# General tiles for the transferred weight groups of a seven-product down projection, and half the finished blocks added to x in DRAM

## The chip, the cores and the metric

The kernel runs on one core of one Trainium2 chip. The metric is the device time of one execution in microseconds (us). The kernel before was timed in three runs: 789.63, 788.41 and 789.20 us, median 789.2. A separate execution, with the hardware profiler on, took 788.42 us; its span from the first to the last instruction is 786.6 us, at a mean granted TensorE clock of 0.99.

Engines: TensorE (PE in the profile; PEld are its weight loads), VectorE (DVE), ScalarE (ACT), GpSimd (POOL) and SyncE (SP). GpSimd and SyncE issue nearly all of the transfers in the part discussed here.

## The reference

One block of a hybrid network: 512 tokens, model width 1024, float32. A gated mix of an mLSTM and a block attention comes first and gives a new x; then follow a second norm and a gated feed-forward, and a last norm. Only the end matters here:

```python
h = modulate(rms_norm(x, norm2_g[l]), sh2, sc2)
f = jax.nn.silu(jnp.einsum('bsd,df->bsf', h, w_gate[l])) * jnp.einsum('bsd,df->bsf', h, w_up[l])
x = x + g2[:, None, :] * jnp.einsum('bsf,fd->bsd', f, w_down[l])
...
return rms_norm(x, normf_g)
```

f is 512 x 2816, w_down is 2816 x 1024.

## The kernel before

**Products in float32r.** Every product is made of three matmuls (`mm3`, L285 to L287): each operand is split into a rounded part ("hi", cast to float32r) and a remainder ("lo"), and hi.hi, hi.lo and lo.hi are accumulated in PSUM. For the weights that is `cvt` (ScalarE casts at L268, DVE subtracts at L270), for the moving or stationary activations `split` (ScalarE at L291, DVE at L292). A weight chunk arrives in a "raw" buffer (4 of them, `load`, SyncE, L182 and L187) and leaves as a pair of "whl" buffers (4 of them, so two chunks).

**Seven products.** Of the 22 row blocks of w_down, 16 are multiplied as a 2 x 2 block matrix in seven products in place of eight. `PRODUCTS = (1, 2, 5, 6, 3, 7, 4)` is their order. Each product has two weight groups of 128 x 2048 (1 MB), so there are 14 groups, g = 0 to 13. A group is 24 matmuls: two halves e (of tokens), four quarters k (512 columns of the group), three matmuls each. Products 5, 7, 6 and 4 need sums of weight blocks; those are made beforehand by DMA in DRAM (tiles `ws`). The other side needs sums of blocks of f, made by DVE (`sum1` to `sum4`) in place, and split group by group (`aparts`). The results sit in three pairs of PSUM banks (yb, xb2, zb): copies are kept (`keep`), finished blocks are summed (`summed`) and added onto x (`onto_x`): DVE scales the block by g2, and GpSimd issues a DMA that adds it to its destination.

**Transferred groups.** Four of the 14 groups (`BY_DMA`) take no part in `cvt`. GpSimd loads the weights with a DMA that rounds them to float32r (`rounded_load`, L217); ScalarE writes the negative of that into a second buffer (`remainder_load`, L223); GpSimd then lets a DMA add the weights once more onto that, which leaves the remainder (L225). In the kernel before these are groups 2, 5, 8 and 12. Both buffers come from the four "raw" ones. In the loop over groups, iteration g first issues `rounded_load(g + 3)` and then `remainder_load(g + 2)`; the load of group 2 stands inside the last gate/up chunk (L1561).

**Order.** The schedule is written by hand: each engine executes its instructions in the order in which the program issues them. In iteration g come the loads of groups g + 2 and g + 3, the two lines just named, and for each half e the entry of `hooks`, the splits and the cast for group g + 1, and the half's 12 matmuls. Tiles of one kind share a number of buffers; a new one takes the buffer that has been free longest, and its first writer waits for the last reader of the tile before. General tiles `T()` (128 x 512, 31 buffers) hold splits, kept copies, x's rows at the end and more; `X()` tiles (8 buffers) mostly hold blocks of f.

**x and the end.** x was written to DRAM earlier (`xkeep`). After the last gate/up chunk its eight quarter rows are fetched into general tiles (L1689), and all eight finished blocks are added onto those. Behind the seven products come six plain row blocks (`PLAIN`, three chunks of two, from `C_PL` on): 8 banks, 24 products of three matmuls a chunk. The first chunk runs whole, the other two are interleaved per output block with the residuals (L1803), the last norm and the stores. Their weights are multiplied by g2 first (`gate_weights`, L244). `fsplit(k)` makes the six splits of f for them; split 0 is made in group 13, 1 and 2 with the first chunk, 3 to 5 after it.

Of the kernel before, what the change touches and what calls it, by code (L numbers as in the profile page):

```python
# [14 lines left out]
ALU = mybir.AluOpType  # L15
# [96 lines left out]
def block_kernel(ctx, tc, x, wall, adaw, pcol, prow, positions, inv_freq, out):  # L112
# [82 lines left out]
    def operand(o, g):  # L195
        p = PRODUCTS[o]
        if p in wsum:
            return wsum[p][blk(g), :]
        return flat(wall, OFF_BLOCKS[{1: 0, 2: 2, 3: 3}[p]] + g * 128 * 2048, [[2048, 128], [1, 2048]])
# [10 lines left out]
    BY_DMA = (2, 5, 8, 12)  # L210

    def rounded_load(g):
        n = C_DN + g
        if g in BY_DMA:
            raws[n] = None
            parts[n] = tuple(wp.tile([128, RAW], F32R, tag="raw", name=nm("wd"), bufs=4)[:, :SIZES[n]] for _ in range(2))
            G.dma_start(parts[n][0], operand(*divmod(g, 2)))  # L217

    def remainder_load(g):
        if g in BY_DMA:  # L220
            hi, lo = parts[C_DN + g]
            for e in range(2):
                A.activation(lo[:, e * 1024:e * 1024 + 1024], hi[:, e * 1024:e * 1024 + 1024].bitcast(F32),  # L223
                             AF.Copy, scale=-1.0)
            G.dma_start(lo, operand(*divmod(g, 2)), accum_op=ALU.add)  # L225
# [1309 lines left out]
    def seven(n):  # L1535
# [24 lines left out]
        if not more:  # L1560
            rounded_load(2)  # L1561
            aparts(0)
# [123 lines left out]
    for i in range(NT):  # L1686
        for q in range(2):
            xr[i][q] = T()
            SP.dma_start(xr[i][q][:], xkeep[i][:, q * 512:q * 512 + 512])  # L1689
# [18 lines left out]
    def onto_x(name, e, i, q):  # L1708
        t = kept[name][e]
        if q:  # L1710
            V.scalar_tensor_tensor(out=t, in0=t, scalar=-1.0, in1=g2row[q][:, :512], op0=ALU.mult, op1=ALU.mult)
        else:
            V.tensor_tensor(out=t, in0=t, in1=g2row[q][:, :512], op=ALU.mult)
        G.dma_start(xr[i][q][:], t, accum_op=ALU.add)

    def pair():
# [11 lines left out]
        (8, 1): lambda: summed("m1", xb2, 0),  # L1728
        (9, 0): lambda: (onto_x("m1", 0, 0, 0), summed("m1", xb2, 1)),
        (9, 1): lambda: onto_x("m1", 1, 1, 0),  # L1730
        (10, 0): lambda: summed("u2", zb, 0),
        (10, 1): lambda: (onto_x("u2", 0, 0, 1), summed("u2", zb, 1)),
        (11, 0): lambda: onto_x("u2", 1, 1, 1),
        (11, 1): lambda: summed("m5", yb, 0),
        (12, 0): lambda: (summed("m5", yb, 1), onto_x("m5", 0, 2, 1)),
        (12, 1): lambda: gate_weights(C_PL, 0),
        (13, 0): lambda: (gate_weights(C_PL, 1), onto_x("m5", 1, 3, 1)),
# [3 lines left out]
    for g in range(groups):  # L1741
# [4 lines left out]
        rounded_load(g + 3)  # L1746
        remainder_load(g + 2)
        wh, wl = parts_of(n)
        for e in range(2):
            hooks.get((g, e), lambda: None)()  # L1750
            if g < groups - 1:
                aparts(2 * g + 2 + e)
            elif e == 0:
                fps[0] = fsplit(0)
            if g + 1 not in BY_DMA:
                cvt(n + 1, e)
            for k in range(4):
                ah, al = (v[:, k % 2, blk(e)] for v in ap[2 * g + k // 2])
                mm3(target[p][e][:], ah, al, wh[:, k, :], wl[:, k, :], p in (1, 2, 5) and g % 2 == 0 and k == 0,
                    g % 2 == 1 and k == 3, True)  # L1760
    nfrow = [T(), T()]
    for q in range(2):
        SP.dma_start(nfrow[q][:, :512], flat(prow, PB + 2 * D + q * 512, [[0, 128], [1, 512]]))
# [10 lines left out]
    for kk in range(2):  # L1774
        if kk:
            mid(C_PL)
        fps[kk + 1] = fsplit(kk + 1)
        for i in range(NT):
            for q in range(2):
                mm3(db[i][q][:], fps[kk][0][:, blk(i)], fps[kk][1][:, blk(i)], ch[0][:, kk, q * 512:(q + 1) * 512],  # L1780
                    ch[1][:, kk, q * 512:(q + 1) * 512], kk == 0, kk == 1 and (i, q) == (NT - 1, 1))
    root_table()
# [3 lines left out]
    for k in range(3, 2 * NP):  # L1786
        fps[k] = fsplit(k)
# [147 lines left out]
```

## Time and profile before

| | us |
|---|---|
| median of three runs | 789.2 |
| the profiled execution | 788.42 |
| its span | 786.6 |
| seven-product down projection (first to last matmul's start) | 648.17 to 742.88 |
| plain products, to the last matmul | 742.88 to 779.58 |

How to read the views used below. A row of the timeline has the start in us from the span's start, the duration, the engine, the line of the kernel, the operation, output<-input by the program's names, and in brackets the idle time before it and what ended that. Matmuls overlap: the distance of two starts is what one costs. A row of the waits has who waited for whom, us in total, times, and the longest. A row of busy time by stretches has from:to, length, each engine's busy time with its number of instructions, the granted clock of TensorE, the mean busy share of the 16 DMA engines, and GB/s. A row of a DMA queue has packets, MB and the time that its packets took as a share of 16 engines. The engines' idle time counts only where it ends last.

### The profile page before, as it was taken

What the parts mean: (1) busy time and instruction counts of PE and PEld (TensorE: products, weight loads), DVE (VectorE), ACT (ScalarE), POOL (GpSimd) and SP (SyncE); (2) the same over time, 40 slices, a digit from 0 to 9 for tenths busy, and PEclk for the clock granted to TensorE, in tenths of its full rate; (3) what the DMA queues carried; (4) which work ended last, traced back from release to release, by engine and by line L of the source; (5) the groups of instructions that cost most, each with busy time, mean ns of one, the idle gap of its engine ahead of it and who ended that gap; (6) DMA issues with size and microseconds to landing.
All of it is one profiled execution on the core that took longest, in us unless ns stands there. A gap on an engine that the chain in (4) does not pass through costs nothing.

```text
span 786.6 us, 12066 instructions
## 1 busy us (share of the span) xinstructions
PE 760.7 (97%) x4587; PEld 660.0 (84%) x4587; DVE 555.6 (71%) x879; ACT 389.3 (49%) x686; POOL 344.9 (44%) x447
## 2 busy tenths in 40 slices
PE   8999999999999999999999999999999999797986
PEld 7789988778887787788889999999999998575865
DVE  5677877665565544488647799898988877656765
ACT  6679743324454444322357545555554554464243
POOL 5484545999856878950002045453653000002200
PEclk9999999999999999999999999999999999898999
DMA  9954325435421422559326438363947456668812
GB/s 337 385 176 153 108 80 175 133 131 215 151 108 55 161 107 107 210 193 322 102 82 215 162 121 240 137 237 112 312 157 205 171 182 194 174 200 233 236 38 108
DMA packets 30041, 136.17 MB, mean 173 GB/s; under 512 B 4120, under 2 KB 4256, under 8 KB 17056
## 3 DMA queue, kind: packets, MB, share of 16 engines
q1 hardware_dynamic: 23680, 105.72, 37.0%
q0 software_dynamic: 4480, 27.26, 14.2%
q10 hardware_dynamic: 1824, 2.43, 1.2%
q8 instruction: 36, 0.59, 0.3%
q14 instruction: 21, 0.17, 0.1%
HBM read 127.01 MB, written 20.97 MB: 188 GB/s over the span
## 4 chain that ended last, share of the span: by engine, by line
PE 82%; DVE 7%; DMA 6%; ACT 2%; issue 2%; SPq 0%; ACTq 0%; DVEq 0%
PE psm L285 12%; PE psm L287 12%; PE psm L286 12%; PE psb L285 6%; PE psb L286 6%; PE psb L287 6%; PE psa L286 5%; PE psa L287 5%; PE psa L285 5%; DMA wd<-ws 2%; DMA t<-in_dram 2%; DVE whl L270 2%; PE psa L655 1%; PE psa L1156 1%; DVE whl L1506 1%
## 5 line engine op out<-in xcount | busy, mean ns | idle before, releaser
L270 DVE TENSOR_TENSOR whl<-raw,whl 128x1024 fp32r<-128x1024 f32 (+2 forms) x92 | 116.5, 1271 | 46.4 <-ACT whl L268 43.7
L268 ACT CAST whl<-raw 128x1024 fp32r<-128x1024 f32 (+2 forms) x91 | 92.6, 1034 | 51.4 <-DVE raw L244 18.7
L338 POOL TENSOR_TENSOR accp<-accp,prod 128x256 f32<-128x256 f32 x112 | 98.6, 880 | 9.3
L1500 ACT CAST whl<-raw 128x1024 fp32r<-128x1024 f32 x57 | 59.8, 1050 | 69.8 <-DVE raw L1490 47.0
L335 POOL TENSOR_SCALAR prod<-ada,cact 128x256 f32<-128x256 f32 x112 | 90.4, 807 | 0.1
L1506 DVE TENSOR_TENSOR whl<-raw,whl 128x1024 fp32r<-128x1024 f32 x57 | 72.6, 1275 | 16.1 <-ACT whl L1500 15.9
L285 PE MATMUL psa<-t,whl 128*128 128x256 f32 x276 | 79.0, 286 | 2.0 <-DVE f L1593 2.0
L287 PE MATMUL psa<-t,whl 128*128 128x256 f32 x276 | 78.1, 283 | 0.0
L286 PE MATMUL psa<-t,whl 128*128 128x256 f32 x276 | 78.1, 283 | 0.0
L285 PE MATMUL psm<-hh,whl 128*128 128x512 f32 x192 | 77.5, 404 | 0.5 <-ACT x L1138 0.5
L285 PE MATMUL psm<-t,whl 128*128 128x256 f32 (+1 forms) x256 | 76.2, 298 | 0.0
L286 PE MATMUL psm<-t,whl 128*128 128x256 f32 (+1 forms) x256 | 75.8, 296 | 0.0
L287 PE MATMUL psm<-t,whl 128*128 128x256 f32 (+1 forms) x256 | 75.8, 296 | 0.0
L287 PE MATMUL psm<-hh,whl 128*128 128x512 f32 x192 | 74.9, 390 | 0.0
L286 PE MATMUL psm<-hh,whl 128*128 128x512 f32 x192 | 74.9, 390 | 0.0
L285 PEld LDWEIGHTS psa<-t,whl 128*128 128x128 f32 x276 | 52.9, 192 | 2.7 <-DVE f L1593 2.6
L286 PEld LDWEIGHTS psa<-t,whl 128*128 128x128 f32 x276 | 53.0, 192 | 0.1
L287 PEld LDWEIGHTS psa<-t,whl 128*128 128x128 f32 x276 | 52.9, 192 | 0.0
L285 PEld LDWEIGHTS psm<-t,whl 128*128 128x128 f32 x256 | 49.0, 191 | 1.4 <-DVE x L1593 0.2
L286 PEld LDWEIGHTS psm<-t,whl 128*128 128x128 f32 x256 | 49.0, 191 | 1.3
L287 PEld LDWEIGHTS psm<-t,whl 128*128 128x128 f32 x256 | 49.0, 191 | 1.3
L335 POOL TENSOR_SCALAR accp<-ada,cact 128x256 f32<-128x256 f32 x16 | 12.1, 757 | 86.5 <-DMA ada<-in_dram 86.5
(493 smaller groups left out, 2045.3 us busy)
## 6 DMA issues: line engine op xcount, KB each, us to landing
raw<-in_dram SPq DMA_DIRECT2D x55, 1024.0 KB, 5.2
ada<-in_dram SPq DMA_DIRECT2D x16, 1024.0 KB, 4.8
ws<-in_dram POOLq DMA_DIRECT2D x6, 2048.0 KB, 14.4
t<-in_dram SPq DMA_DIRECT2D x32, 256.0 KB, 6.2
raw<-ws SPq DMA_DIRECT2D x6, 1024.0 KB, 6.8
ws<-ws POOLq DMA_DIRECT2D x2, 2048.0 KB, 12.2
wd<-in_dram POOLq DMA_DIRECT2D x4, 1024.0 KB, 6.5
wd<-ws POOLq DMA_DIRECT2D x4, 1024.0 KB, 7.9
```

Source lines behind the costliest of these rows:

```text
L268: (eng.tensor_copy if eng else A.copy)(hi[:, s], raws[n][:, s])
L270: (eng or V).tensor_tensor(out=lo[:, s], in0=raws[n][:, s], in1=hi[:, s].bitcast(F32), op=ALU.subtract)
L285: PE.matmul(o, lh, rh, start=start, stop=False, skip_group_check=again)
L286: PE.matmul(o, lh, rl, start=False, stop=False, skip_group_check=again)
L287: PE.matmul(o, ll, rh, start=False, stop=stop, skip_group_check=again)
L335: G.tensor_scalar(t[:], rv[:, k, :], cact[:, k:k + 1], 1.0, op0=ALU.mult, op1=ALU.mult)
L338: G.tensor_tensor(out=p[:], in0=p[:], in1=t[:], op=ALU.add)
L655: PE.matmul(g1[m][:], w[:, blk(m)], h[:], start=k == 0 and e == 0, stop=k == KD - 1 and e == 2)
L1156: PE.matmul(bs[e][:, o:o + n], qp[a][r, blk(i)], kp[b][r, :n], start=g == 0, stop=g == 2)
L1500: A.copy(hi, src)
L1506: V.tensor_tensor(out=lo, in0=src, in1=hi.bitcast(F32), op=ALU.subtract)
```

## The change

The transferred groups become 4, 7, 10 and 13. Each is held in eight general tiles (four quarters of the rounded part, four of the remainder) and transferred in quarters of 256 KB. The rounded load is issued at the head of iteration g - 4, the negation and the adding load in the second half of iteration g - 3. Group 2 is an ordinary group now, and the early load in the last gate/up chunk is gone. Of x's rows, two are fetched into `X()` tiles before the seven products, two in group 12, and four after the first plain chunk's first half; the four finished blocks of the first 256 tokens (m1 and u2) are added onto `xkeep` in DRAM, ahead of that fetch. The hooks of groups 8 to 13 are regrouped, and the splits for the plain products come one step earlier. The load of the last norm's row moves behind the fetch of x.

```diff
@@ -192,11 +192,12 @@
 
     wsum = {p: dq.tile([256, 2048], F32, tag=f"ws{p}", name=nm("ws")) for p in (5, 7, 6, 4)}
 
-    def operand(o, g):
+    def operand(o, g, k=None):
         p = PRODUCTS[o]
+        c, w = (0, 2048) if k is None else (k * 512, 512)
         if p in wsum:
-            return wsum[p][blk(g), :]
-        return flat(wall, OFF_BLOCKS[{1: 0, 2: 2, 3: 3}[p]] + g * 128 * 2048, [[2048, 128], [1, 2048]])
+            return wsum[p][blk(g), c:c + w]
+        return flat(wall, OFF_BLOCKS[{1: 0, 2: 2, 3: 3}[p]] + g * 128 * 2048 + c, [[2048, 128], [1, w]])
 
     def weight_sums():
         for p, q, b in ((5, None, (0, 0)), (7, None, (1, 1)), (6, 7, (0, 0)), (4, 6, (1, 0))):
@@ -207,22 +208,21 @@
 
     wsums = weight_sums()
 
-    BY_DMA = (2, 5, 8, 12)
+    BY_DMA = (4, 7, 10, 13)
+    cast = {}
 
     def rounded_load(g):
-        n = C_DN + g
         if g in BY_DMA:
-            raws[n] = None
-            parts[n] = tuple(wp.tile([128, RAW], F32R, tag="raw", name=nm("wd"), bufs=4)[:, :SIZES[n]] for _ in range(2))
-            G.dma_start(parts[n][0], operand(*divmod(g, 2)))
+            cast[g] = [[T(dt=F32R)[:] for _ in range(4)] for _ in range(2)]
+            for k in range(4):
+                G.dma_start(cast[g][0][k], operand(*divmod(g, 2), k))
 
     def remainder_load(g):
         if g in BY_DMA:
-            hi, lo = parts[C_DN + g]
-            for e in range(2):
-                A.activation(lo[:, e * 1024:e * 1024 + 1024], hi[:, e * 1024:e * 1024 + 1024].bitcast(F32),
-                             AF.Copy, scale=-1.0)
-            G.dma_start(lo, operand(*divmod(g, 2)), accum_op=ALU.add)
+            for k in range(4):
+                hi, lo = (t[k] for t in cast[g])
+                A.activation(lo, hi.bitcast(F32), AF.Copy, scale=-1.0)
+                G.dma_start(lo, operand(*divmod(g, 2), k), accum_op=ALU.add)
 
     gated = set()
 
@@ -1558,7 +1558,6 @@
         make(n, (7, 4))
         load(n + 3)
         if not more:
-            rounded_load(2)
             aparts(0)
         product(n, 5)
         A.copy(m5, c["z"])
@@ -1683,10 +1682,12 @@
     aparts(1)
     finish4(LAST)
     late(LAST)
-    for i in range(NT):
-        for q in range(2):
-            xr[i][q] = T()
-            SP.dma_start(xr[i][q][:], xkeep[i][:, q * 512:q * 512 + 512])
+    def fetch_x(i, q, alloc=T):
+        xr[i][q] = alloc()
+        SP.dma_start(xr[i][q][:], xkeep[i][:, q * 512:q * 512 + 512])
+
+    for i in (3, 2):
+        fetch_x(i, 1, X)
 
     while bg[0]:
         spend(0.5)
@@ -1711,7 +1712,7 @@
             V.scalar_tensor_tensor(out=t, in0=t, scalar=-1.0, in1=g2row[q][:, :512], op0=ALU.mult, op1=ALU.mult)
         else:
             V.tensor_tensor(out=t, in0=t, in1=g2row[q][:, :512], op=ALU.mult)
-        G.dma_start(xr[i][q][:], t, accum_op=ALU.add)
+        G.dma_start(xr[i][q][:] if i > 1 else xkeep[i][:, q * 512:q * 512 + 512], t, accum_op=ALU.add)
 
     def pair():
         return [T()[:] for _ in range(2)]
@@ -1725,16 +1726,16 @@
         (6, 0): lambda: (keep("m5", zb, pair()), sum4(0)),
         (7, 0): lambda: sum4(1),
         (8, 0): lambda: keep("u2", yb, pair()),
-        (8, 1): lambda: summed("m1", xb2, 0),
-        (9, 0): lambda: (onto_x("m1", 0, 0, 0), summed("m1", xb2, 1)),
-        (9, 1): lambda: onto_x("m1", 1, 1, 0),
+        (9, 0): lambda: (summed("m1", xb2, 0), summed("m1", xb2, 1)),
+        (9, 1): lambda: (onto_x("m1", 0, 0, 0), onto_x("m1", 1, 1, 0)),
         (10, 0): lambda: summed("u2", zb, 0),
-        (10, 1): lambda: (onto_x("u2", 0, 0, 1), summed("u2", zb, 1)),
-        (11, 0): lambda: onto_x("u2", 1, 1, 1),
+        (10, 1): lambda: summed("u2", zb, 1),
+        (11, 0): lambda: onto_x("u2", 0, 0, 1),
         (11, 1): lambda: summed("m5", yb, 0),
-        (12, 0): lambda: (summed("m5", yb, 1), onto_x("m5", 0, 2, 1)),
-        (12, 1): lambda: gate_weights(C_PL, 0),
-        (13, 0): lambda: (gate_weights(C_PL, 1), onto_x("m5", 1, 3, 1)),
+        (12, 0): lambda: (summed("m5", yb, 1), onto_x("u2", 1, 1, 1), fetch_x(2, 0), fetch_x(3, 0)),
+        (12, 1): lambda: (onto_x("m5", 1, 3, 1), gate_weights(C_PL, 0)),
+        (13, 0): lambda: gate_weights(C_PL, 1),
+        (13, 1): lambda: onto_x("m5", 0, 2, 1),
     }
 
     groups = 2 * len(PRODUCTS)
@@ -1743,24 +1744,25 @@
         p = PRODUCTS[g // 2]
         for e in (2, 3):
             load(n + e)
-        rounded_load(g + 3)
-        remainder_load(g + 2)
-        wh, wl = parts_of(n)
+        rounded_load(g + 4)
+        if g in BY_DMA:
+            wh, wl = cast[g]
+        else:
+            wh, wl = ([t[:, k, :] for k in range(4)] for t in parts_of(n))
         for e in range(2):
             hooks.get((g, e), lambda: None)()
+            if e:
+                remainder_load(g + 3)
             if g < groups - 1:
                 aparts(2 * g + 2 + e)
-            elif e == 0:
-                fps[0] = fsplit(0)
+            else:
+                fps[e] = fsplit(e)
             if g + 1 not in BY_DMA:
                 cvt(n + 1, e)
             for k in range(4):
                 ah, al = (v[:, k % 2, blk(e)] for v in ap[2 * g + k // 2])
-                mm3(target[p][e][:], ah, al, wh[:, k, :], wl[:, k, :], p in (1, 2, 5) and g % 2 == 0 and k == 0,
+                mm3(target[p][e][:], ah, al, wh[k], wl[k], p in (1, 2, 5) and g % 2 == 0 and k == 0,
                     g % 2 == 1 and k == 3, True)
-    nfrow = [T(), T()]
-    for q in range(2):
-        SP.dma_start(nfrow[q][:, :512], flat(prow, PB + 2 * D + q * 512, [[0, 128], [1, 512]]))
     for e in range(2):
         t = T()
         V.tensor_tensor(out=t[:], in0=yb[e][:], in1=g2row[0][:, :512], op=ALU.mult)
@@ -1774,16 +1776,23 @@
     for kk in range(2):
         if kk:
             mid(C_PL)
-        fps[kk + 1] = fsplit(kk + 1)
+        fps[kk + 2] = fsplit(kk + 2)
         for i in range(NT):
             for q in range(2):
                 mm3(db[i][q][:], fps[kk][0][:, blk(i)], fps[kk][1][:, blk(i)], ch[0][:, kk, q * 512:(q + 1) * 512],
                     ch[1][:, kk, q * 512:(q + 1) * 512], kk == 0, kk == 1 and (i, q) == (NT - 1, 1))
+        if kk == 0:
+            for i in range(2):
+                for q in range(2):
+                    fetch_x(i, q)
+            nfrow = [T(), T()]
+            for q in range(2):
+                SP.dma_start(nfrow[q][:, :512], flat(prow, PB + 2 * D + q * 512, [[0, 128], [1, 512]]))
     root_table()
     last = [begin(C_PL + NP - 2)]
     mid(C_PL + NP - 2)
     last.append(begin(C_PL + NP - 1))
-    for k in range(3, 2 * NP):
+    for k in range(4, 2 * NP):
         fps[k] = fsplit(k)
 
     def tail(e, i, cuts, fresh=False):
```

## The prediction

> **What bounds the kernel now.** I read the page first, then the busy time by stretches over the last 140 us, then TensorE's matmuls in order of time around each gap, then the waits.
>
> ```profile
> span 786.6 us, 12066 instructions
> core 0: us, PE busy (x) PEld busy (x) DVE busy (x) ACT busy (x) POOL busy (x), PEclk, DMA share, GB/s
> 648.17:742.88 94.71, 83.81 (x338) 66.27 (x337) 61.10 (x77) 44.62 (x61) 10.41 (x13) 0.93 0.72 207
> 742.88:779.70 36.82, 33.70 (x157) 27.37 (x155) 25.20 (x53) 14.92 (x31) 3.06 (x3) 1.00 0.30 79
> 779.70:786.60 6.90, 0.16 (x2) 0.00 (x0) 2.53 (x9) 1.87 (x5) 0.00 (x0) 0.82 0.41 152
> 669.96:684.38 14.42, 8.72 (x26) 6.48 (x25) 9.71 (x12) 9.00 (x12) 0.87 (x1) 0.76 0.64 175
> 689.82:702.29 12.47, 11.64 (x49) 8.85 (x48) 6.00 (x7) 7.53 (x11) 0.88 (x1) 1.00 0.87 235
> 718.61:732.00 13.39, 9.02 (x25) 6.30 (x25) 7.35 (x10) 9.42 (x13) 2.62 (x3) 0.75 0.87 186
> ```
>
> The first stretch is the seven-product down projection (14 groups), the second the plain products behind it, the third what follows the last matmul. The matmuls themselves show where time is lost:
>
> ```profile
> 648.17 0.40 PE L285 MATMUL psa<-whl,t 128*128 128x512 f32 x1
> 659.08 0.39 PE L285 MATMUL psm<-wd,t 128*128 128x512 f32 x1
> 669.73 0.39 PE L287 MATMUL psm<-whl,t 128*128 128x512 f32 x1
> 675.35 0.80 PE L285 MATMUL psb<-whl,t 128*128 128x512 f32 x1 [5.23 <-ACT whl L268]
> 718.38 0.39 PE L287 MATMUL psa<-whl,t 128*128 128x512 f32 x1
> 722.46 0.59 PE L285 MATMUL psa<-whl,t 128*128 128x512 f32 x1 [3.69 <-ACT whl L268]
> 742.88 0.39 PE L285 MATMUL psa<-whl,t 128*128 128x512 f32 x1
> 748.55 0.39 PE L286 MATMUL psa<-whl,t 128*128 128x512 f32 x1
> 749.52 0.50 PE L287 MATMUL psa<-whl,t 128*128 128x512 f32 x1 [0.58 <-DVE t L292]
> 755.12 0.39 PE L287 MATMUL psa<-whl,t 128*128 128x512 f32 x1
> 757.25 0.50 PE L285 MATMUL psa<-whl,t 128*128 128x512 f32 x1 [1.74 <-ACT t L291]
> 758.78 0.51 PE L287 MATMUL psa<-whl,t 128*128 128x512 f32 x1 [0.80 <-DVE t L292]
> 779.58 0.28 PE L287 MATMUL psa<-whl,t 128*128 128x256 f32 x1
> ```
>
> Groups 0 and 1 are 2 x 24 = 48 matmuls and take 659.08 - 648.17 = 10.91 us, a pitch of 0.2273 us and 5.455 us a group. Fourteen groups at that pitch are 76.37 us; the stretch takes 94.71, so **18.34 us** are lost in it. Three places hold all of it: group 4 takes 14.42 us (8.97 lost), groups 6 and 7 take 12.47 (1.56), group 11 takes 13.39 (7.93). In the first and third of these the granted clock also falls to 0.76 and 0.75: the gaps of 5.6 and 4.1 us are followed by matmuls at half pace (0.80 us long instead of 0.39). The gap of 2.1 us at 755.12 has no such tail (clock 1.00 in its stretch). So a long gap costs its length and 3 to 4 us more.
>
> Why the gaps come:
>
> ```profile
> ACT wd L223 <- DMA wd<-ws: 19.0, 2, 9.9
> ACT wd L223 <- DMA wd<-in_dram: 8.3, 1, 8.3
> POOL wd L217 <- PE psb L287: 14.2, 1, 14.2
> POOL wd L217 <- PE psm L286: 12.9, 1, 12.9
> 664.62 0.55 POOL L217 DMA_DIRECT2D wd<-ws  x1 [12.86 <-PE psm L286]
> 671.84 2.00 ACT L223 ACTIVATE wd<-wd 128x1024 fp32r<-128x1024 f32 x2 [9.04 <-DMA wd<-ws]
> 674.14 0.87 POOL L225 DMA_DIRECT2D wd<-ws  x1 [8.96 <-ACT wd L223]
> ```
>
> Group 5 is transferred by GpSimd. Its rounded load (L217) wants a "raw" buffer that group 2's matmuls still read, so it goes out at 664.62 only. ScalarE meets the negation of that load (L223) one group later, sits 9.04 us until 671.84, and behind it in its queue stand the splits and the casts of group 4. TensorE waits for those (5.23 us, released by L268). Groups 8 and 12 repeat it. TensorE bounds the stage; what holds it is a late transfer, seen through a blocked ScalarE.
>
> **The change part by part.**
>
> *Buffers and lead.* The four transferred groups become 4, 7, 10, 13. Each gets eight general tiles, not two of the four raw buffers, and its load is issued four groups ahead; the negation stands in the second half of the group three ahead. Let TensorE start group g at 648.17 + 5.455 g. The negations then stand, at the latest, at 656.4, 672.7, 689.1 and 705.5 us, and the remainders are wanted at 670.0, 686.4, 702.7 and 719.1, 13.6 us later (10.9 before). What has to fit:
>
> ```profile
> q0 software_dynamic: 144, 1.05, 72.9%
> q0 software_dynamic: 144, 1.05, 81.6%
> q0 software_dynamic: 432, 0.79, 53.9%
> DMA to landing us min/median/max: 7.9/7.9/8.2
> t<-xk SPq DMA_DIRECT2D x8, 256.0 KB, 4.5
> 638.16 5.67 SPq L1689 DMA_DIRECT2D t<-xk  x8
> ```
>
> These are the GpSimd queue's packets in three stretches: one 1 MB accumulation in 651.0 to 658.9 (72.9% of 7.9 us = 5.76 us of all engines), one 1 MB rounded load in 686.5 to 690.4 (81.6% of 3.9 = 3.18 us), three 256 KB accumulations in 744 to 752 (53.9% of 8 = 4.31, 1.44 each). Then the landing times of the 1 MB remainders (L225), and x's eight fetches, with their median landing and their issues. Four quarters of an accumulation are 4 x 1.44 = 5.75 us: cutting the transfer in four costs the engines nothing. A remainder's queue time is 5.76 of 7.9 us, so some 2.1 us are start and landing. From the first negation: 0.6 (negation) + 2.1 + 5.75 = 8.5 us for the last quarter. Issue, four times 0.87 us, runs beside the transfer. It is wanted 13.6 + 2.0 us after (a quarter serves 0.68 us of each half), so some 7 us remain.
>
> The rounded loads: GpSimd issues them in queue order, the one of group 7 behind the remainder of group 4. That ends at 656.4 + 8.5 = 664.9; the load is 3.2 us more, so 668.1, and ScalarE wants it at 672.7. The margin is 4.6 us, and the same for groups 10 and 13. The load of group 4 uses the tiles that x's eight fetches used, which were free from 638.16 to 643.8: 12 us ahead. One load of SyncE between costs some 3.2 us (1 MB as above), which still fits; two do not. ScalarE itself runs ahead of TensorE here, since a transferred group needs no cast. So all three losses go: **-18.3 us**.
>
> *What is late next.* DVE has 61.1 us and ScalarE 44.6 of work in this stage, 80% and 58% of 76.4. The DMA engines are nearer: 0.72 x 94.71 = 68 us, and the bytes stay the same, so 89% of 76.4. This is the cover that could fail (below).
>
> *General tiles.* Sixteen of 31 are held when two transferred groups overlap, 4 by the kept m5 and u2 and 8 by splits: 28. The eight that x held till the end are gone (two now in x tiles, two fetched at group 12, four after the first plain product). Nothing waits, by that count, with three spare. ScalarE's negations become four of about 0.6 us in place of two of 1.05, some 0.3 us a group more on an engine that is 58% busy.
>
> *Half the finished blocks onto x in DRAM.* The same eight accumulations of 256 KB. Four now end in DRAM and are read back by SyncE, four fetches of 256 KB, in the plain stage, where the share of DMA is 0.30. The trace has no accumulation into DRAM. The nearest rows, accumulations into SBUF (L1714, below), landed after 3.6 to 10.8 us. The last one into DRAM is issued in group 12, about 715; by the later end it has landed at 726 and is read back (4.5) at 731. The first residual comes after 48 + 24 plain matmuls, about 741. I take the later end; no cost by either. SyncE's fetches wait for those accumulations, and behind them stand only the normf rows, wanted as late.
>
> *SyncE's order.* One x fetch waits for the last block of f (about 650), and behind it stands the load of group 3, cast at 660: 10 us for a landing of 5 to 7 (the rounded load issued at 664.62 let ScalarE go at 671.84, 7.2 us later). Group 2's weights are now an ordinary load ahead of it, with a raw buffer of its own. The two fetches of group 12 stand before the last plain chunk's load, which is gated some 12 us later. No cost.
>
> *Splits of the plain stage.* The splits 1, 2, 3 each move one step earlier. The gaps there are 0.74 us at 748.55 (split 1's remainder), 1.90 at 755.12 and 1.08 behind it (split 3, released by L291 and L292). 132 whole matmuls at 0.2273 us and 24 of half width at half that are 32.7 us of the 36.8. With split 1 done within group 13 and split 3 before the cast of the last chunk, these 3.72 us lose their cause. What is late next is DVE's run of gate, remainder and split for that chunk, which by my count ends within a microsecond of its use. I keep 0.7 us: **-3.0 us**.
>
> *Sum.* The profiled execution took 788.42 us, span 786.6. 788.42 - 18.3 - 3.0 = 767.1; I add 0.2 for small waits: **767.3 us**. The runs shown have a median of 789.2, 0.8 above the profiled one, within their own spread (788.41 to 789.63).
>
> **The rivals.**
>
> *Crowded DMA.* At 89% the engines have queues, and two or three of SyncE's loads may stand ahead of a rounded load; 4.6 us of margin go, ScalarE blocks as before. For: the stretches with stalls show 0.87 now. Against: the loads of SyncE can go earlier too, as the raw buffers are theirs alone. One long gap costs as group 4's did, 9 us: 776.
>
> *Quarters in series.* If each 256 KB transfer paid its whole way alone, four would take 4 x 3.6 us:
>
> ```profile
> 733.79 0.87 POOL L1714 DMA_DIRECT2D t<-t  x1 [5.42 <-DVE t L1711]
> DMA to landing us min/median/max: 3.6/8.8/10.8
> 743.77 1.77 POOL L1767 DMA_DIRECT2D t<-t  x2 [2.60 <-DVE t L1766]
> DMA to landing us min/median/max: 6.6/6.8/7.1
> ```
>
> The one issued at 733.79 landed in 3.6 us, with little else moving. 14.4 us against 13.6 would make each of the four remainders about 1 us late, and each load of 14.4 us instead of 3.2 would run into ScalarE's margin: 11 - 4.6, some 6 us a group for three groups, partly absorbed; about 12 us, 779. Against: the two of L1767 went out 0.6 us apart and both landed within 7.1, and the three in that stretch overlapped at 1.44 each. The Trainium skill, "DMA: Bandwidth & Descriptors", in its section on the anatomy of one DMA gives about 2.0 us fixed plus bytes / 436e3 per transfer and asks in its rules for 1 MiB or more; by that alone a load in quarters would be an estimated 4 x 2.6 = 10.4 us in series, not 4.4. The trace agrees for a lone transfer, not for overlapping ones.
>
> *Plain stage keeps its gaps.* DVE's chain bounds it whatever the order of splits: 770.
>
> *It doesn't do what it says.* TensorE waits as long for casts whose loads SyncE brings late, since those loads now share the engines with more lead traffic: 788.
>
> *Slower: tiles run out.* With 28 of 31 held, ScalarE's splits for the next half get a tile only when TensorE lets go of one in the same half. Then each half exposes a split and its remainder:
>
> ```profile
> L292 DVE TENSOR_TENSOR t<-f,t 128x512 fp32r<-128x512 f32 x27 | 18.3, 685 | 29.2 <-ACT t L291 29.2
> L291 ACT CAST t<-f 128x512 fp32r<-128x512 f32 x26 | 15.5, 616 | 1.7 <-DVE f L1669 1.7
> ```
>
> 0.62 + 0.69 = 1.3 us, 28 halves: 36 us, 767 + 36 = 803. It turns slower than before from 0.8 us a half on (22 / 28). It needs all 31 held from group 0, against 28 at the peak, groups 9 and 10.
>
> **How the numbers follow.** Forecast 0.68, crowded DMA 0.12, quarters in series 0.06, plain stage keeps its gaps 0.07, no change 0.03, slower 0.04. Below: all 22.1 us gone is 766.3, less the spread of a run, 765.3. Above: up to one long gap, 776; the cases beyond hold about 0.13. A change under 0.2% can't be told from none here. Faster 0.93, same 0.03, slower 0.04.
>
> **What would show it.** Right: matmuls at 0.227 us from 648 to about 725 without a gap, granted clock 1.00 there, ScalarE's wait for "wd" gone, last matmul near 758. Wrong: a gap before group 5, 8 or 11 (a rounded load late) or before 4, 7, 10, 13 (a remainder late), released by a DMA; a DMA share near 1; splits waiting for TensorE; gaps at the plain stage's second and third part.

## The result, and the profile after

The changed kernel takes 768.67 us (median of four runs, 768.61 to 769.23) against 788.89 before (the three runs named above and a fourth): 20.2 us less, a ratio of 0.974 (95% interval 0.973 to 0.976). The forecast was 767.3, in a range of 765.3 to 776.0. The profiled execution took 769.23 us, 19.2 less than the profiled one of before; the stages below are compared between these two. One execution of kernel 4 in the table below took 1058.92 us at a granted clock of 0.655 and is left out of its median, which would be 767.8 with it, the figure that later expectations name.

The page's span, and the busy time by stretches (columns as before); the stretches are the same three stages, then the 18 us around the first long transfer:

```profile
span 767.4 us, 12165 instructions
...
648.17:727.82 79.65, 77.43 (x339) 62.84 (x337) 62.05 (x78) 44.99 (x68) 25.81 (x35) 1.00 0.95 266
727.82:760.62 32.80, 32.80 (x157) 27.60 (x155) 24.10 (x51) 14.41 (x30) 2.99 (x3) 1.00 0.26 68
760.62:767.40 6.78, 0.15 (x2) 0.00 (x0) 2.53 (x9) 1.86 (x5) 0.00 (x0) 0.83 0.42 156
...
655.00:673.20 18.20, 17.44 (x77) 14.08 (x75) 14.58 (x16) 9.84 (x16) 5.73 (x8) 1.00 1.03 321
```

The seven products take 79.65 us in place of 94.71: **15.06 us**. The plain products begin at 727.82 and their last matmul starts at 760.49, 32.67 us in place of 36.70: **4.03 us**. The rest stands where it stood. The granted clock is 1.00 in both stages: no gap is long enough to leave matmuls at half pace behind it. The DMA share of the first stage has gone from 0.72 to 0.95, and the engines are full from 655 to 673 (1.03; above 1 because the records of packets overlap a little).

Fourteen groups at full pitch are 76.37 us, so 3.28 are still lost, nearly all of it in three gaps. The timeline of TensorE shows where they are; the waits of ScalarE and its negations (L224) show what they stand behind:

```profile
672.05 0.39 PE L285 MATMUL psb<-t,t 128*128 128x512 f32 x1
673.23 0.50 PE L286 MATMUL psb<-t,t 128*128 128x512 f32 x1 [0.79 <-DMA t<-ws]
...
678.07 0.49 PE L285 MATMUL psb<-whl,t 128*128 128x512 f32 x1
679.33 0.50 PE L286 MATMUL psb<-whl,t 128*128 128x512 f32 x1 [0.77 <-DVE whl L270]
...
695.57 0.40 PE L285 MATMUL psb<-whl,t 128*128 128x512 f32 x1
696.63 0.50 PE L286 MATMUL psb<-whl,t 128*128 128x512 f32 x1 [0.66 <-DVE whl L270]
```

```profile
ACT t L224 <- DMA t<-ws: 17.0, 7, 6.7
...
654.57 2.19 ACT L224 ACTIVATE t<-t 128x512 fp32r<-128x512 f32 x4
673.92 2.64 ACT L224 ACTIVATE t<-t 128x512 fp32r<-128x512 f32 x4 [6.73 <-DMA t<-ws]
690.23 0.63 ACT L224 ACTIVATE t<-t 128x512 fp32r<-128x512 f32 x1 [3.59 <-DMA t<-ws]
```

Group 4 waits once for its own remainder. Groups 5 and 8 are ordinary groups: VectorE's remainder of the weights (L270) comes late because ScalarE's cast ahead of it did, and ScalarE stood before a negation whose rounded load had not landed. It is the old chain (late transfer, blocked ScalarE, starved TensorE), at about 1 us a time in place of 8 or 9. The next rows show those transfers: the issues of SyncE and GpSimd, then the landing times of the remainder of group 4 (L225) and of the rounded load of group 7 (L218).

```profile
650.81 0.42 SPq L182 DMA_DIRECT2D raw<-in_dram  x1
651.34 3.98 SPq L182 DMA_DIRECT2D raw<-ws  x2
...
655.49 3.56 POOL L225 DMA_DIRECT2D t<-ws  x4 [13.83 <-ACT t L224]
657.67 3.55 POOL L218 DMA_DIRECT2D t<-ws  x4
...
DMA to landing us min/median/max: 8.2/12.8/16.1
...
DMA to landing us min/median/max: 16.2/16.4/16.6
```

The last quarter of the remainder needs 16.1 us, where the 1 MB transfer of before needed 7.9; the load behind it lands at 674 to 676, not 668.1. The remainder starts late and then goes slowly. GpSimd issues its quarters from 655.49 on, but up to 660.4 only SyncE's queue moves packets (94.3% of the engines' time from 655.5 on): the loads that went out just before come first. From then to 673.2 the two queues share full engines (60.9% for GpSimd's, 45.8% for SyncE's).

Why the engines are full, from the DMA queues in the seven products (packets, MB, share of 16 engines), first before, then after:

```profile
q0 software_dynamic: 1728, 8.65, 41.3%
q1 hardware_dynamic: 1508, 10.88, 30.7%
```

```profile
q0 software_dynamic: 4752, 8.65, 53.3%
q1 hardware_dynamic: 2523, 12.47, 41.3%
...
t<-xk SPq DMA_DIRECT2D x6, 256.0 KB, 5.0
```

GpSimd's queue (q0) moves the same 8.65 MB, but takes 0.533 x 79.65 = 42.5 us of all engines in place of 0.413 x 94.71 = 39.1. SyncE's (q1) takes 32.9 in place of 29.1, for 1.6 MB more: six fetches of x's rows into general tiles, and one into an `X()` tile, are now in this stage. Together that is 7.2 us more engine time, in a stage 15 us shorter.

### The profile page after: what moved, and what is told of

Its sections match the earlier page's. It is cut to its first block, busy times and chain, and to the rows that moved or that the text cites. A ratio compares the mean times of both kernels' runs of the same rounds, so it can differ in the third digit from the quotient of the medians.

```text
span 767.4 us, 12165 instructions
## 1 busy us (share of the span) xinstructions
PE 753.5 (98%) x4587; PEld 657.4 (86%) x4587; DVE 555.1 (72%) x879; ACT 390.7 (51%) x694; POOL 361.8 (47%) x471
## 4 chain that ended last, share of the span: by engine, by line
PE 85%; issue 4%; DVE 4%; DMA 4%; ACT 1%; POOL 0%; POOLq 0%; DVEq 0%; ACTq 0%; SPq 0%
PE psm L285 12%; PE psm L286 12%; PE psm L287 12%; PE psb L285 6%; PE psb L286 6%; PE psb L287 6%; PE psa L285 5%; PE psa L286 5%; PE psa L287 5%; DMA t<-ws 3%; PE psa L655 1%; DMA t<-in_dram 1%; PE psa L1156 1%; DVE whl L1506 1%; PE psb L553 1%
## 5 line engine op out<-in xcount | busy, mean ns | idle before, releaser
L270 DVE TENSOR_TENSOR whl<-raw,whl 128x1024 fp32r<-128x1024 f32 (+2 forms) x92 | 116.2, 1267 | 45.4 <-ACT whl L268 42.7
```

What stands on the lines that cost most here:

```text
L270: (eng or V).tensor_tensor(out=lo[:, s], in0=raws[n][:, s], in1=hi[:, s].bitcast(F32), op=ALU.subtract)
```

## The experiments

Stage lengths are from the profile of each kernel, seven products and plain products to the last matmul's start; times are medians, ratios are to the kernel before on the same chip, with the 95% interval.

| kernel | us | ratio | seven products | plain |
|---|---|---|---|---|
| before | 788.89 | 1 | 94.71 | 36.70 |
| after | 768.67 | 0.974 (0.973 to 0.976) | 79.65 | 32.67 |
| 1 plain splits as before | 772.87 | 0.979 (0.978 to 0.981) | 79.70 | 36.39 |
| 2 before, with the new splits only | 784.54 | 0.994 (0.992 to 0.995) | 94.14 | 33.38 |
| 3 before, with the new x rows only | 791.92 | 1.003 (1.002 to 1.005) | 93.04 | 39.62 |
| 4 short lead | 766.93 | 0.971 (0.969 to 0.973) | 79.22 | 32.80 |
| 5 short lead, raw buffers | 783.02 | 0.992 (0.990 to 0.995) | 92.61 | 34.33 |
| 6 short lead, old groups | 776.10 | 0.984 (0.982 to 0.985) | 87.31 | 32.67 |
| 7 long lead, old groups | 781.87 | 0.990 (0.988 to 0.992) | 93.43 | 32.67 |
| 8 early x fetches later | 769.61 | 0.975 (0.974 to 0.977) | 79.74 | 32.67 |
| 9 SyncE's loads in quarters | 767.97 | 0.973 (0.971 to 0.974) | 78.17 | 32.68 |
| 10 group 4's remainder early | 767.16 | 0.972 (0.970 to 0.973) | 77.66 | 32.67 |
| 11 negation behind the cast | 767.31 | 0.973 (0.971 to 0.974) | 77.91 | 32.67 |
| 12 three of these together | 765.85 | 0.971 (0.969 to 0.972) | 76.22 | 32.67 |

The intervals of kernels 9, 10 and 11 each overlap that of the change, so what each is worth is read from its stage and its gaps.

### 1 and 2: the splits

```diff
-            else:
-                fps[e] = fsplit(e)
+            elif e == 0:
+                fps[0] = fsplit(0)
...
-        fps[kk + 2] = fsplit(kk + 2)
+        fps[kk + 1] = fsplit(kk + 1)
...
-    for k in range(4, 2 * NP):
+    for k in range(3, 2 * NP):
```

> The changed kernel with the splits of the plain products where they were (split 0 in group 13, 1 and 2 with the first chunk, 3 to 5 after it). My step: the earlier splits are what closed the plain stage's gaps (36.8 us before, 32.8 after). Expected 771.5 to 772.7, gaps of 0.5 to 2 us at the second and third part of the plain stage. Rival: it was the chain before the stage that got ahead, and the splits' places matter little: 768.7 to 769.7.

> The kernel before with the splits of the plain products one step earlier and nothing else. Alone they should take 2.5 to 4 us off the plain stage: 785 to 786.5. If DVE is so far behind at group 13 that one more split there delays the first chunk, 787 to 789.

Kernel 1 is the changed one with this edit, kernel 2 the one before with the reverse. The gaps return in the first, at the same places in the stage. The two longer ones are as long as before (2.13 and 1.20 us from start to start; the first of them is shown), the other is 0.67 in place of 0.97:

```profile
734.14 0.50 PE L287 MATMUL psa<-whl,t 128*128 128x512 f32 x1 [0.29 <-DVE t L292]
...
741.84 0.50 PE L285 MATMUL psa<-whl,t 128*128 128x512 f32 x1 [1.74 <-ACT t L291]
```

They cost 4.2 us between the medians (3.7 in the stage), 0.2 more than the top of the expectation. In the second the stage falls by 3.32 and keeps one gap of 0.79; the time is a little below the range, 4.95 us under the 789.49 of the kernel before on that chip. The splits are worth 3.3 us of the stage by themselves, and 4 to 5 us between medians.

### 3: x's rows alone

Kernel 3 is the one before with the changed x handling: two early fetches into `X()` tiles, two in group 12, four in the plain stage, half the finished blocks onto x in DRAM, the regrouped hooks, and the load of the last norm's row behind the fetch.

```diff
-            xr[i][q] = T()
-            SP.dma_start(xr[i][q][:], xkeep[i][:, q * 512:q * 512 + 512])
+    for i in (3, 2):
+        fetch_x(i, 1, X)
...
-        G.dma_start(xr[i][q][:], t, accum_op=ALU.add)
+        G.dma_start(xr[i][q][:] if i > 1 else xkeep[i][:, q * 512:q * 512 + 512], t, accum_op=ALU.add)
```

> The kernel before with only the handling of x as in the changed kernel (two fetches into x tiles, two in group 12, four after the first plain chunk's first half, four finished blocks added to x in DRAM, hooks regrouped; transferred groups 2, 5, 8 and 12 and their lead as before). My step: no cost and no gain by itself, 788 to 790. If it frees the engines or the queues where the stalls are, 784 to 787; if the accumulations in DRAM come late for the residuals, 790 to 795 with waits of DVE for them.

It is a little slower, 0.2 to 0.5%, and above the expected range. Its profiled execution, 789.49, is the fastest of its six, so the trace shows the effects at their smallest. The rows come from the timeline, from the landing times of two transfers (group 2's remainder, L225, and a plain chunk's weights, L187, issued at 737.27), and the last from the busy time by stretches.

```profile
650.24 0.33 SPq L1688 DMA_DIRECT2D x<-xk  x1
650.62 0.42 SPq L182 DMA_DIRECT2D raw<-in_dram  x1
...
DMA to landing us min/median/max: 12.5/12.5/12.5
...
663.25 0.79 PE L286 MATMUL psm<-wd,t 128*128 128x512 f32 x1 [3.98 <-DMA wd<-in_dram]
...
747.02 1.29 DVE L244 TENSOR_TENSOR raw<-raw,v 128x512 f32<-128x512 f32 x2 [0.67 <-DMA raw<-in_dram]
...
DMA to landing us min/median/max: 9.6/9.6/9.6
...
741.02:780.80 39.78, 35.34 (x157) 28.50 (x155) 25.83 (x54) 14.96 (x31) 3.60 (x4) 0.96 0.40 119
```

There are two effects. The second early fetch waits for its `X()` tile until 650.24, and the load of group 3 behind it, which went out at 643.92 before, now meets the remainder of group 2: 12.5 us to land, and a stall in group 2. (The stage is 1.7 us shorter all the same, as the stall of group 4 is gone with it: group 4 now starts later than its casts.) And six of the fetches go out around the plain chunk's load, which takes 9.6 us to land; VectorE waits for it, and the gap before split 1's remainder grows from 0.97 to 2.28 us. The plain stage is 2.9 us longer. The other 1.6 are matmuls at half pace (clock 0.96) behind the two later gaps, which are as long as in the kernel before, where the clock stayed at 1.00.

No wait of VectorE for an accumulation into DRAM stands behind this, which was the reason given for 790 to 795. In the changed kernel the cost is covered, and not by the earlier splits: kernel 1 has the splits of before and the new x rows, and its plain stage takes 36.39. What differs is when SyncE gets to its issues: there the plain chunk's load goes out at 711.9 and the four fetches from 715.5 on, 16 and 12 us ahead of the stage, here at 737.3 and 737.9, 4 and 3 us ahead. That this is the cover is argued, not tested.

### 4 to 7: lead, tiles, groups

Kernel 4 has the old lead:

```diff
-        rounded_load(g + 4)
+        rounded_load(g + 3)
+        remainder_load(g + 2)
...
-            if e:
-                remainder_load(g + 3)
```

> The changed kernel with one edit: the lead of the kernel before (rounded load in the group three ahead, negation and adding load at the head of the group two ahead), general tiles kept. If the tiles alone did it (a rounded load that doesn't wait for matmuls to leave raw buffers), 769 to 771. If the lead is needed too, as I hold (a remainder took up to 16 us to land and now has 10.9 us), groups 4 and 7 wait for remainders, 3 to 6 us each with half clock behind: 776 to 783.

The time is that of the changed kernel or a little less (the intervals overlap), so the expectation that the lead is needed was wrong. By its place in the program group 4's remainder is half a group, 2.7 us, later than with the long lead; by the timeline it goes out 1.2 us later:

```profile
656.72 3.56 POOL L225 DMA_DIRECT2D t<-ws  x4 [13.40 <-ACT t L224]
```

ScalarE runs ahead of TensorE until something holds it, and GpSimd's issue waits for ScalarE; the place in the program is not the place in time.

Kernel 5 is kernel 4 with two raw buffers for each transferred group, and transfers of 1 MB, as before:

```diff
-            cast[g] = [[T(dt=F32R)[:] for _ in range(4)] for _ in range(2)]
-            for k in range(4):
-                G.dma_start(cast[g][0][k], operand(*divmod(g, 2), k))
+            parts[n] = tuple(wp.tile([128, RAW], F32R, tag="raw", name=nm("wd"), bufs=4)[:, :SIZES[n]] for _ in range(2))
+            G.dma_start(parts[n][0], operand(*divmod(g, 2)))
```

> The changed kernel with groups 4, 7, 10 and 13, but each held in two of the four raw buffers again, moved in 1 MB, its rounded load issued three and its negation two groups ahead, as before (that lead alone, with general tiles, gave 767.8). Theory 'the tiles did it': the rounded load of group 7 again waits for the matmuls of group 4 that read its buffers, so ScalarE blocks and TensorE stalls for 8 to 9 us at two or three places: 780 to 790 us, with gaps of over 3 us released by casts of L268. Rival 'it was the choice of groups, the x rows and the regrouped work': 768 to 771 us.

```profile
673.70 0.55 POOL L217 DMA_DIRECT2D wd<-ws  x1 [11.62 <-DVE whl L270]
678.93 2.01 ACT L223 ACTIVATE wd<-wd 128x1024 fp32r<-128x1024 f32 x2 [8.40 <-DMA wd<-ws]
682.45 0.50 PE L285 MATMUL psa<-whl,t 128*128 128x512 f32 x1 [1.05 <-ACT whl L268]
...
704.04 0.50 PE L285 MATMUL psb<-whl,t 128*128 128x512 f32 x1 [2.34 <-ACT whl L268]
...
726.17 0.76 PE L285 MATMUL psa<-whl,t 128*128 128x512 f32 x1 [3.11 <-ACT t L291]
```

The whole chain is back in its first three rows: the load waits 11.62 us for a buffer, ScalarE 8.40 for the load, TensorE for ScalarE. The seven products are 13.4 us longer than kernel 4's, at clock 0.93. **With these groups, the tiles carry the gain.** The edit changes the size of the transfers too, and no run has general tiles with 1 MB; that it is the buffers is read from the wait of 11.62 us. What was off in the expectation is the size of each stall, 2.2 to 3.6 us where 8 to 9 were expected, the slow matmuls behind them apart, and who ends the waits: the buffer comes from VectorE's remainder (L270) of an ordinary group, not from the matmuls of group 4, and the longest gap is ended by a split (L291), not by a cast.

Kernels 6 and 7 keep the tiles and take the old groups, with the short and with the long lead (in both, group 2's negation stands at the head of group 0):

```diff
-    BY_DMA = (4, 7, 10, 13)
+    BY_DMA = (2, 5, 8, 12)
...
+            rounded_load(2)
             aparts(0)
```

> The changed kernel with general tiles and quarters, but groups 2, 5, 8 and 12 and the lead of three and two groups as before (the lead alone gave 767.8). Theory 'the tiles did it, whichever the groups': 767 to 770 us, no gap over 2 us in the seven products. Rival 'the shift of the groups matters too': group 2's remainder, then beside the loads behind the x fetch, comes late as it did when the x rows were moved alone (12.5 us to land, 4 us lost with half-paced matmuls behind): 772 us or more.

> The changed kernel, lead of four and three groups included, with groups 2, 5, 8 and 12 (group 2's load in the last gate/up chunk, its negation at the head of group 0). The same groups with the short lead gave 776.1 and lost most in group 12, whose remainder went out at 705.0 behind two accumulations onto x that wait for VectorE in GpSimd's queue until 703.7. Theory 'place in the queue': the longer lead doesn't help there, since the remainder still stands behind these two: out at 700 to 705, a gap of over 1.5 us in group 12 released by a DMA, 772 to 777 us. Rival 'the lead absorbs it': 767 to 770 us, no such gap.

The choice of groups matters, 9 us at the short lead, but not where the rival had it: group 2 has no gap in kernel 6, and group 12 has the longest. The rows are of kernel 7: GpSimd and then TensorE in group 12, then ScalarE and TensorE in group 3.

```profile
710.44 1.78 POOL L1716 DMA_DIRECT2D xk<-v  x2 [18.98 <-DVE v L1715]
711.86 3.90 POOL L225 DMA_DIRECT2D t<-ws  x4
...
727.75 0.50 PE L286 MATMUL psa<-t,t 128*128 128x512 f32 x1 [2.58 <-DMA t<-ws]
730.02 0.79 PE L286 MATMUL psa<-t,t 128*128 128x512 f32 x1 [1.30 <-DMA t<-ws]
```

```profile
669.87 0.63 ACT L224 ACTIVATE t<-t 128x512 fp32r<-128x512 f32 x1 [2.54 <-DMA t<-ws]
...
672.01 0.79 PE L285 MATMUL psm<-whl,t 128*128 128x512 f32 x1 [5.84 <-ACT whl L268]
```

Group 12's remainder stands in GpSimd's queue behind two accumulations onto x, which wait 18.98 us for VectorE; it goes out with them whatever the lead, and TensorE loses the same two gaps (2.97 and 1.70 us from start to start) as in kernel 6 (2.95 and 1.69). That part of the expectation held, only that the issue is at 711.86 and not at 700 to 705, since the stage has lost time by then. The time did not hold: 781.87 is 5 us above the range. The longer lead puts group 5's negation ahead of the second cast of group 3, while its load still lands (the last quarter is negated at 669.87), so ScalarE blocks earlier, and TensorE stands idle for 5.84 us. In ScalarE's queue, a lead for one instruction is a block for those behind it.

### 8 to 10: why the transfers land late

Kernel 8 moves the two early fetches to group 8, so that no load of SyncE is held until 650 (load 3 goes out at 642.35). Kernel 9 cuts SyncE's loads in this stage into four. Kernel 10 issues group 4's remainder in group 0's second half.

```diff
-    for i in (3, 2):
-        fetch_x(i, 1, X)
...
-        (8, 0): lambda: keep("u2", yb, pair()),
+        (8, 0): lambda: (keep("u2", yb, pair()), fetch_x(3, 1, X), fetch_x(2, 1, X)),
```

```diff
-            SP.dma_start(raws[n][:, :2048], operand(*divmod(n - C_DN, 2)))
+            for k in range(4):
+                SP.dma_start(raws[n][:, k * 512:k * 512 + 512], operand(*divmod(n - C_DN, 2), k))
```

```diff
-                remainder_load(g + 3)
+                remainder_load(g + (3 if g else 4))
```

> The changed kernel with one edit: the two early fetches of x (into x tiles, before group 0) move into group 8. What is left of the stalls in the changed kernel is 3.3 us, at groups 4, 5 and 8. Theory 'pile-up': SyncE stands at the second fetch until 650.4 and then issues the loads of groups 3, 5 and 6 within 5 us, which hold all DMA engines from 651 to 660, so group 4's remainder (issued 655.5 to 657.1) starts at 660 and lands at 673.2, and group 7's load behind it at 673.9. It expects loads 3 and 5 several us earlier, the remainder landed before 668, the gaps in groups 4 and 5 (2.2 us) gone, and 766.3 to 766.8 us. Theory 'packets': the quarters' 2 KB packets take turns with SyncE's 8 KB packets and lose, whenever the loads go out; it expects little, 768.0 to 768.7.

> The changed kernel with one edit: SyncE's loads of the ordinary groups go in four quarters with 2 KB packets, as GpSimd's do. Theory 'packets' expects GpSimd's queue to win turns: at equal packet sizes an accumulating packet (178 ns) waits for one of 100 ns and not of 325 ns, so group 4's remainder lands in about 10 us in place of 16 and most of the 3.3 us goes: 765.8 to 767. Theory 'pile-up' expects the same 3 MB in front and some 20% more engine time for them (2 KB packets take 100 ns, four of them 400 against 325): 768.7 to 771.

> The changed kernel with one edit: group 4's negation and adding load move from group 1's second half to group 0's second half (its rounded load landed at 645). Both theories expect its issue at about 650, ahead of most of SyncE's loads, landing before 664, group 7's load before 668 and groups 4 and 5 without a gap: 766.3 to 767.0. If group 4's remainder isn't what makes group 7 late, the gap of group 5 (1.3 us) stays: 767.7.

These are the landing times of group 4's remainder and then of group 7's rounded load, in kernels 8, 9 and 10 (in the changed kernel 8.2/12.8/16.1 and 16.2/16.4/16.6):

```profile
DMA to landing us min/median/max: 6.8/9.7/14.9
DMA to landing us min/median/max: 15.4/15.6/15.8
```

```profile
DMA to landing us min/median/max: 8.2/10.6/12.7
DMA to landing us min/median/max: 13.6/14.8/16.1
```

```profile
DMA to landing us min/median/max: 4.5/8.9/13.7
DMA to landing us min/median/max: 17.2/20.9/22.2
```

Without the pile-up the remainder is 1 us earlier. That is enough for group 4, whose gap is gone, but the gaps in groups 5 and 8 are longer (3.2 us over the pitch in all, 2.8 in the changed kernel), and the time is no better: **the held fetch is not the cause of what is lost**. One load of SyncE still goes out just ahead of the remainder, and from 655.5 to 659.6 again only SyncE's queue moves packets. With SyncE's loads in quarters the remainder is 3.4 us earlier than in the changed kernel, the gaps in groups 4 and 8 go, and the one in group 5 stays (767.97, between the two expectations). With an early issue the remainder is there in time, and of the three gaps only group 5's is left (767.16, just above the better expectation), but the load of group 7 behind it, issued 6 us sooner, still lands its last quarter at 675. So it does in all three, at 675 to 676: the engines are full there, and it is the order of the transfers that can be chosen, not their sum. That SyncE's 8 KB packets take turns from GpSimd's 2 KB ones would fit kernel 9, but no run separates it from the sum.

### 11 and 12: taking the rest

Kernel 11 puts the negation behind the cast of the same half; kernel 12 does this, and the edits of kernels 9 and 10.

```diff
-            if e:
-                remainder_load(g + 3)
             if g < groups - 1:
                 aparts(2 * g + 2 + e)
...
                 cvt(n + 1, e)
+            if e:
+                remainder_load(g + 3)
```

> The changed kernel with the negation of a transferred group put behind the cast of the same half instead of ahead of the splits and that cast. Theory 'ScalarE blocked': the gaps of 1.03 us in group 5 and 0.83 us in group 8 come from casts that stand behind a negation that waits for its load; they go, the one of 0.95 us in group 4 stays: 766.5 to 767.2 us against 768.7. Rival 'the casts wait for their own raw loads, as all loads land late on full DMA engines': 768.2 to 769.2 us, the gaps where they were.

> The negation behind the cast, group 4's remainder issued in group 0's second half, and SyncE's group loads in quarters of 256 KB, together. If the three gaps have the causes named (late remainder of group 4; casts behind blocked negations), none is left in the seven products: 768.7 - 3.1 = 765.5 us, 765.2 to 766.4 with the small steps. Rival 'the full DMA engines only move the wait to another group': 766.8 to 768 us.

In kernel 11 the gaps in groups 5 and 8 are gone and group 4's is left, alone, released by its remainder: the place of the negation in ScalarE's queue was their cause. The time is 0.1 us above the expected range. The remaining gap, and below it kernel 12 by stretches:

```profile
673.21 0.50 PE L286 MATMUL psb<-t,t 128*128 128x512 f32 x1 [1.27 <-DMA t<-ws]
```

```profile
647.85:724.07 76.22, 76.22 (x339) 63.11 (x337) 62.23 (x78) 45.15 (x68) 26.02 (x35) 1.00 1.02 280
724.07:756.90 32.83, 32.83 (x157) 27.62 (x155) 24.10 (x51) 14.44 (x30) 2.81 (x3) 1.00 0.24 64
```

TensorE is busy for the whole of both stages, with the DMA engines full on average (1.02) in the first. It has the lowest median of the study, 765.85 us, and its interval lies below that of the change.

## Why the prediction was right

**What bounds.** Right, and shown by kernel 5: with the raw buffers back, the late load, the blocked ScalarE and the stalls are back.

**Buffers and lead, -18.3 us.** The mechanism was right and the size was not: 15.06 measured. The step that was mis-sized is "0.6 (negation) + 2.1 + 5.75 = 8.5 us for the last quarter" and the load behind it at 668.1. From the first negation at 654.57 the last quarter took 18.6 us (16.1 from its own issue), and the load landed at 674 to 676. The sum had no term for loads of SyncE that go out just before, and these held the engines for the first 5 us. Two more reasons stand in the queues. "Cutting the transfer in four costs the engines nothing" holds for accumulations (1.44 us each) and not for the rounded loads: the one of group 4 takes 51.0% of 8 us, 4.08 us in place of 3.18 (group 8's, the one that the prediction measured) or 2.6 (group 5's in the kernel before, 75.0% of the 3.5 us from 668.0):

```profile
q0 software_dynamic: 576, 1.05, 51.0%
```

And "the bytes stay the same, so 89%" missed the x rows: 95% measured, and full where it counts. The Trainium skill, "DMA: Bandwidth & Descriptors", asks in its rules for transfers of 1 MiB or more. For the rounded load the trace agrees, at least 28% more engine time in quarters. For SyncE's loads kernel 9 shows no loss of time, though its queue takes 35.0 us of the engines there (44.8% of 78.17) in place of 32.9.

**The lead.** The prediction put lead and tiles into one term. Kernel 4 shows that the lead adds nothing measurable with these groups, and kernel 7 that it can cost. The choice of groups was not priced at all; kernel 6 gives it 9 us, and with the long lead of the change the old groups end at 781.87, outside the range. That the chosen groups were good ones was luck as far as the prediction goes.

**Margin.** That one load of SyncE between would fit and two would not was the right warning: three of its loads go out between 650.8 and 655, and ScalarE waits 6.73 us for group 7's load. But a late load of this size cost TensorE about 1 us and no half pace, not the 9 us of the rival "crowded DMA". That rival came true in its cause and not in its price. By the prediction's own list, gaps behind late transfers and a DMA share near 1 were signs of being wrong; both are there, but cost 3.3 us in all where it priced a single gap at 9. "Quarters in series" did not come true: the quarters of the remainder land about 3 us apart, yet only with full engines, and the four of group 4's rounded load, with little else moving, land after 4.6 us (median). (The lone accumulation of 256 KB took 3.6 us, 1 us above the 2.6 of the prediction's estimate, so the agreement claimed there was a loose one.)

**Tiles.** No wait for a tile shows in the waits of ScalarE in this stage; the count of 28 of 31 was enough, and the slower rival did not occur. SyncE's fetches of x do wait for TensorE (12.7 us in three waits), at no cost, since they still go out well ahead of their use.

**x in DRAM, no cost.** The accumulations into DRAM landed in 5.3 to 9.1 us, inside the bounds of 3.6 and 10.8, and no residual waited. (The trace of before does hold accumulations into DRAM, against what the prediction says: four of 2 MB for the weight sums, L205, landing after 13.5 to 17.3 us. They are eight times as large and would not have changed the bounds.) But the fetches were not in the plain stage, as the prediction had them: SyncE runs ahead of TensorE and issued the last four from 716.9 on, 11 us before that stage. The landings of L1715 and the issues:

```profile
DMA to landing us min/median/max: 5.3/7.5/9.1
...
716.90 7.70 SPq L1687 DMA_DIRECT2D t<-xk  x4
```

By itself this part costs (kernel 3). In the sum it was covered.

**SyncE's order, no cost.** Right in the sum, by kernel 8. In kernel 3 the same held fetch went with a stall, where group 2 was a transferred group and its remainder met the late load.

**Splits, -3.0 us.** 4.03 measured. The 0.7 us kept for VectorE's run behind them was not lost.

**Sum.** -18.3 - 3.0 + 0.2 = -21.1 was forecast for the profiled execution; -15.06 - 4.03 = -19.1 came of the two stages, and 0.1 elsewhere. The two errors, 3.2 us too much and 1.0 too little, have opposite signs, and 2 us is what is left of them; that they offset each other is luck.

## What to carry to other kernels

Give a transfer that an engine's queue will wait for buffers of its own before giving it lead: with buffers shared, the queue stalled behind the load (kernel 5), and a longer lead in an engine's queue moved the wait ahead of work that was ready (kernel 7). Before counting on a transfer's landing time, sum the engine time of everything that the idle queues will issue by then, since SyncE and GpSimd run ahead of TensorE here, and what was issued first moved first. Full DMA engines need not cost anything (kernel 12): put what is wanted first into the queue first, and put a waiting instruction behind the ready ones.

## What was not expected of the hardware

A rounded load of 1 MB took 2.6 to 3.2 us of the 16 engines whole and 4.08 in quarters, while an accumulation took 5.76 whole and 1.44 a quarter. The half pace of TensorE came after a gap of 3.50 us (kernel 5, the matmul at 726.17 took 0.76 us), and also after two shorter ones that followed each other: in kernel 7 the matmul behind the gap of 2.97 us still took 0.50 us, the one behind the next gap of 1.70 us took 0.79. The Trainium skill, "TensorE: Matmul & The Clock Gate", in its part on the clock gate lets the clock fall after an idle window of about 3.4 us. The gap in kernel 5 agrees. The pairs of kernel 7 and of kernel 6 (2.95 and 1.69 us, then 0.80) show that gaps below that length can do it when they stand close together. The length alone does not settle it: in kernel 3 the matmul behind a gap of 3.81 us (at 720.74) still took 0.50 us, and the pair of 2.13 and 1.20 us in its plain stage halved the pace for 3.4 us, while the same pair in the kernel before did not. What decides between these is open.
